# The last step of a mixture of experts: the accumulated rows read from POOL's queue, and the tokens finished in two halves

## Chip, cores, metric

The kernel runs on one core of a Trainium2 chip. The metric is the device time of one launch in microseconds (us). Three runs of the kernel before gave 2003.7, 2014.76 and 2016.17 us: a median of 2014.76 us. PE is the matmul engine, DVE the vector engine, ACT the scalar engine, POOL the GpSimd engine, and SP the queue that issues most DMAs.

## What is computed

Two blocks, one after the other, on 512 tokens of width 1024 in fp32. The first is a gated delta rule with a convolution branch and then a mixture of experts, the second a state-space mixer with a feed-forward net. The change lies where the mixture of experts ends and the second block begins:

```python
def moe_ffn(h, router_w, router_bias, w_gate, w_up, w_down, s_gate, s_up, s_down):
    ...
    out = lax.map(expert_block, (slot_tok.reshape(n_blocks, MOE_BLOCK), block_exp))
    weighted = (out.reshape(n_slots, d) * slot_w[:, None]).astype(h.dtype)
    routed = jnp.zeros((t + 1, d), h.dtype).at[slot_tok].add(weighted)[:t]
    return (routed + swiglu(hf, s_gate, s_up, s_down)).reshape(bsz, n, d)
...
        x = x + gt2 * moe_ffn(...)
    return rmsnorm(x, g_final)
...
        xn = rmsnorm_2(h, norm_mix_g[l])
```

So each token's row is the sum of its residual, its shared expert's row and the rows of six routed experts. Two norms follow at once: the first block's last, and the second block's first.

## The kernel before, in words

The 64 experts are taken in blocks of up to 128 slots (`blocks`, line 1642). For each block SP loads three tiles of 1 MB of weights per expert (`load`, line 1525), POOL gathers the tokens' rows (`gather`, line 1593), and `ffn` computes: PE turns the rows, DVE and ACT copy them out, PE multiplies gate and up (`gu`), ACT and DVE form the gated product, PE multiplies down (`py`), and DVE writes the scaled result `y` (line 1631). `scatter` (line 1639) then adds `y` to a table in DRAM: an indirect DMA that POOL issues, with addition in the DMA. There are two such tables, `yacc[0]` and `yacc[1]`, which the scatters use in turn. `yacc[0]` was filled with the residual rows at the start.

The last block has no scatter. At its place in the program the kernel does the following:

- `sums(0)` reads the table `yacc[0]` into two slots of the weights' ring (line 1686), four DMAs of 512 KB, one for each tile of 128 tokens. The remaining scatters are issued, and `sums(1)` reads `yacc[1]` in the same way.
- `ysh`, which appears in the trace as the tile `h`, holds the shared expert's rows, four tiles of 128 tokens by 1024 in SBUF. POOL adds the four tiles of the first sum to it (line 1667).
- `ffn` computes the last block, and `beyond` (line 1706) is a loop on the device for experts with more tokens than planned. Its count `nov` is read by every engine (line 1709). In this run the body is never entered, but all engines meet at its entry (line 1710), where SP first waits for the DMAs and engines whose work precedes the loop in the program.
- After the loop the second sum is added: tiles 0 and 1 by DVE, tiles 2 and 3 by POOL (line 1672). `combine` (line 1690) builds one-hot matrices `oh` from the last block's token numbers (lines 1695 and 1698), multiplies each with `y` on PE (tile `pc`, in the trace `pce`, eight of 128x512), and DVE adds each to `h` (line 1704).

Then the second block normalises `h`: ACT squares (line 2278), DVE multiplies by the norm's weight (line 2271), ACT squares that (line 2272), DVE computes the reciprocal roots, and PE turns the tiles (`ptn`) for the first product (`psi`).

A scheduler of the framework sets each engine's order within the program's dependences. Each engine runs its own list in order. A dependence is a semaphore wait in front of an instruction, so everything behind it on that engine waits as well. After the last block's weights SP has the reads of line 1686, and then the loads `wraw` and `wri` of the second block's weights (`w_in`, line 2082), which ACT and DVE split into two parts (lines 273 and 274).

## Time and profile before

| what | us |
|---|---|
| median of three runs | 2014.76 |
| the profiled execution, by its own time | 2013.86 |
| span of its trace | 2012.0 |
| from the first read of a table (1191.0) to the first `xnl` of the second block (1234.3) | 43.3 |

The profile is one execution. A timeline row gives the start in us from the span's start, the duration, the engine, the line and the operation with its tiles, output first. The chain of waits follows the work that ended last back through whatever released it. A "to landing" figure is the time from a DMA's issue to its completion.

### The profile page before, as it was taken

How to read it: one execution, taken by the hardware profiler on the slowest of the kernel's cores; microseconds unless marked ns; L12 is line 12 of the kernel's file. 1: busy time of each engine (PE TensorE's matmuls, PEld its weight loads, DVE VectorE, ACT ScalarE, POOL GpSimd, SP SyncE). 2: the span in 40 equal slices, each digit the busy share in tenths (PEclk: the TensorE clock that was granted, in tenths of full speed). 3: DMA queues.
4: the chain of work that ended last, by engine and by line, in shares of the span. 5: the costliest groups of instructions: out<-in, count | busy, mean ns of one | idle time of the engine just before them, and what ended most of it. 6: DMA issues, size and time to landing. Idle time of an engine off the chain costs nothing.

```text
span 2012.0 us, 24236 instructions
## 1 busy us (share of the span) xinstructions
PE 1832.7 (91%) x8481; PEld 1240.3 (62%) x8481; DVE 991.9 (49%) x2219; ACT 596.6 (30%) x1124; POOL 505.7 (25%) x408
## 2 busy tenths in 40 slices
PE   5897789987888999989999987999999999999998
PEld 3686557875643333333333335888888788888886
DVE  4689955667866222352222227776423453323352
ACT  5443311113423111111111114433423344323341
POOL 1314343542322222212221225342001113101300
PEclk9998889998989999999999997999999999999999
DMA  8354353226487999999999983332323423233241
GB/s 313 119 185 154 89 163 105 77 72 220 155 315 281 354 366 350 346 397 384 367 368 368 376 316 111 113 107 79 113 89 95 140 85 105 89 94 100 79 141 43
DMA packets 135555, 393.64 MB, mean 196 GB/s; under 512 B 46899, under 2 KB 59443, under 8 KB 109064
## 3 DMA queue, kind: packets, MB, share of 16 engines
q1 hardware_dynamic: 116664, 364.45, 51.2%
q0 software_dynamic: 11856, 26.83, 5.4%
q10 hardware_dynamic: 6912, 0.79, 0.3%
q8 instruction: 68, 1.11, 0.2%
q14 instruction: 55, 0.45, 0.1%
HBM read 365.19 MB, written 38.54 MB: 201 GB/s over the span
## 4 chain that ended last, share of the span: by engine, by line
PE 70%; DVE 14%; DMA 10%; ACT 3%; issue 2%; POOL 1%; SPq 0%; ACTq 0%; another core or an unknown queue 0%; DVEq 0%; POOLq 0%
PE psi L139 12%; PE gub L139 11%; PE pof L139 9%; PE psf L139 9%; PE pyb L139 7%; DMA ewrank<-ew 5%; PE psco L139 2%; DVE cfa L746 2%; PE poo L139 2%; PE pt_xb L142 1%; PE pxca L139 1%; PE psga L139 1%; PE psgb L139 1%; PE pxv L139 1%; PE psp L139 1%
## 5 line engine op out<-in xcount | busy, mean ns | idle before, releaser
L139 PE MATMUL gub<-ewrank,xTb 128*64 128x512 f32 (+5 forms) x960 | 266.3, 595 | 0.8 <-DMA ewrank<-ew 0.6
L274 DVE TENSOR_TENSOR wlo<-wraw,whi 128x1024 fp32r<-128x1024 f32 (+1 forms) x102 | 119.8, 1175 | 144.0 <-ACT whi L273 143.2
L139 PEld LDWEIGHTS gub<-ewrank,xTb 128*64 128x64 f32 (+5 forms) x960 | 88.9, 140 | 158.7 <-issue 146.1
L273 ACT CAST whi<-wraw 128x1024 fp32r<-128x1024 f32 (+1 forms) x115 | 113.9, 990 | 217.9 <-PE psi L139 50.5
L139 PE MATMUL pyb<-ewrank,hTb 128*64 128x512 f32 (+5 forms) x440 | 153.4, 612 | 2.4 <-ACT hTb L1622 0.5
L139 PE MATMUL psi<-xnh,whi 128*128 128x512 f32 (+1 forms) x368 | 141.5, 386 | 0.0
L139 PE MATMUL psi<-xnl,whi 128*128 128x512 f32 (+1 forms) x368 | 141.5, 385 | 0.0
L1617 DVE SCALAR_TENSOR_TENSOR hb<-gub,tw,sgb 128x256 f32<-128x256 f32 (+5 forms) x38 | 18.3, 482 | 229.5 <-ACT sgb L1615 229.5
L1341 ACT ACTIVATE xTb<-pt_xb,B,A 128x128 f32<-128x128 f32 (+5 forms) x168 | 74.0, 445 | 179.7 <-DVE xTb L1343 176.6
L1639 POOL DMA_INDIRECT yacc<-yb,tok x61 | 86.1, 1411 | 159.0 <-DVE yb L1631 108.3
L1593 POOL DMA_INDIRECT X<-hrow,tok x38 | 39.6, 1042 | 294.8 <-PE pt_xb L142 289.2
L139 PE MATMUL psi<-xnh,wlo 128*128 128x512 f32 (+1 forms) x296 | 113.2, 383 | 0.0
L1343 DVE TENSOR_SCALAR xTb<-pt_xb,A,B 128x128 f32<-128x128 f32 (+5 forms) x168 | 65.5, 392 | 89.2 <-PE pt_xb L142 52.0
L2433 POOL TENSOR_TENSOR fr<-fr 128x512 f32<-128x512 f32 x32 | 48.6, 1519 | 238.2 <-ACT fr L2432 238.2
L139 PE MATMUL psf<-xml,whi 128*128 128x512 f32 (+1 forms) x272 | 102.5, 377 | 0.2 <-DVE xml L274 0.2
L139 PE MATMUL psf<-xmh,whi 128*128 128x512 f32 (+1 forms) x272 | 102.5, 377 | 0.2 <-ACT xmh L273 0.2
L139 PE MATMUL psf<-xmh,wlo 128*128 128x512 f32 (+1 forms) x272 | 102.4, 377 | 0.0
L1631 DVE TENSOR_TENSOR yb<-pyb,gt 128x512 f32<-128x512 f32 (+5 forms) x84 | 57.9, 690 | 73.7 <-PE pyb L139 73.6
L139 PEld LDWEIGHTS pyb<-ewrank,hTb 128*64 128x64 f32 (+5 forms) x440 | 46.6, 143 | 74.6 <-issue 64.7
L1615 ACT ACTIVATE sgb<-gub 128x256 f32<-128x256 f32 (+5 forms) x42 | 16.0, 381 | 258.3 <-PE gub L139 258.3
L139 PEld LDWEIGHTS psi<-xnh,whi 128*128 128x128 f32 x368 | 69.6, 190 | 13.9 <-issue 0.2
L139 PEld LDWEIGHTS psi<-xnl,whi 128*128 128x128 f32 x368 | 69.7, 189 | 13.5
(755 smaller groups left out, 4041.9 us busy)
## 6 DMA issues: line engine op xcount, KB each, us to landing
ewrank<-ew SPq DMA_DIRECT2D x168, 1024.0 KB
wraw<-w_in SPq DMA_DIRECT2D x59, 512.0 KB
wraw<-ff SPq DMA_DIRECT2D x32, 512.0 KB
wf<-ff SPq DMA_DIRECT2D x64, 256.0 KB
wm<-w_mod SPq DMA_DIRECT2D x28, 512.0 KB
ewfix<-ew SPq DMA_DIRECT2D x12, 1024.0 KB
ewx<-ew SPq DMA_DIRECT2D x12, 1024.0 KB
wm<-w_mod SPq DMA_DIRECT2D x10, 1024.0 KB
```

The lines of the kernel that those rows point to most:

```text
L139: return self._done(self.eng.matmul(out, lhsT, rhs, **kw), rate, rhs)
L142: return self._done(self.eng.transpose(out, in_, ident), 0.00118, ident)
L273: nc.scalar.copy(hi, raw)
L274: (eng or nc.vector).tensor_tensor(lo, raw, hi.bitcast(F32), ALU.subtract)
L746: V.scalar_tensor_tensor(a[:, r0 * 64:r1 * 64], y[:, (r0 + o) * 64:(r1 + o) * 64], w[:, j, 15 + o:16 + o], a[:, r0 * 64:r1 * 64], ALU.mult ...
L1341: nc.scalar.activation(dst(c), pt[:, i, :], AF.Identity, scale=sa, bias=sb)
L1343: nc.vector.tensor_scalar(dst(c), pt[:, i, :], sa, sb, ALU.mult, ALU.add)
L1593: self.k.nc.gpsimd.indirect_dma_start(out=X[0:idx.shape[0]], out_offset=None, in_=self.hrow, in_offset=bass.IndirectOffsetOnAxis(ap=idx, a ...
L1617: nc.vector.scalar_tensor_tensor(h[0:n], gu[0:n, 256:512], wslot[0:n], sg[0:n], ALU.mult, ALU.mult)
L1631: nc.vector.tensor_tensor(y[0:n, cs], py[0:n], self.gt2[0:n, cs], ALU.mult)
L1639: self.k.nc.gpsimd.indirect_dma_start(out=self.yacc[1 - self.nsc % 2], out_offset=bass.IndirectOffsetOnAxis(ap=idx, axis=0), in_=y[a:a + n ...
L2433: nc.gpsimd.tensor_tensor(r, r, r, ALU.mult)
```

## The change

Both reads are issued by POOL in place of SP: two DMAs of 1 MB for each sum in place of four of 512 KB. POOL adds the first sum to tiles 0 and 1 alone. The one-hot matrices of the last block are built before its `ffn`, in the buffer of an earlier block's gathered rows (`Xt[1]`, in the listing `X_4568`). After the loop DVE adds the second sum to tiles 0 and 1, and `combine` finishes these two. Then DVE adds both sums to tiles 2 and 3, and `combine` finishes those. POOL has no addition after the loop.

```diff
--- before.py
+++ after.py
@@ -1663,14 +1663,20 @@
                 while pend:
                     self.scatter(*pend.pop(0))
                 s1 = self.sums(1)
-                for t in range(4):
+                for t in range(2):
                     self.k.nc.gpsimd.tensor_tensor(self.ysh[:, t, :], self.ysh[:, t, :], s0[t], ALU.add)
+                oh = self.ones_at(bp, self.tok[:, b:b + 1], rows, "e")
             y = self.ffn(bp, ps, ws, Xs[n], (self.twf if n < NFIX else self.tw)[:, b:b + 1], rows, f"b{b}")
             if n == len(BLOCKS) - 1:
                 self.beyond(bp, ps)
-                for t in range(4):
-                    (self.k.nc.gpsimd if t > 1 else self.k.nc.vector).tensor_tensor(self.ysh[:, t, :], self.ysh[:, t, :], s1[t], ALU.add)
-                self.combine(bp, ps, y, self.tok[:, b:b + 1], rows, "e")
+                add = lambda t, s: self.k.nc.vector.tensor_tensor(self.ysh[:, t, :], self.ysh[:, t, :], s[t], ALU.add)
+                for t in (0, 1):
+                    add(t, s1)
+                self.combine(ps, y, oh, rows, "e", (0, 1))
+                for s in (s0, s1):
+                    for t in (2, 3):
+                        add(t, s)
+                self.combine(ps, y, oh, rows, "e", (2, 3))
                 break
             part = self.parts(n)
             pend.append((y, part))
@@ -1682,26 +1688,30 @@
     def sums(self, i):
 
         s = [self.slot(f"sum{i}{j}").rearrange("p (t d) -> p t d", t=2) for j in range(2)]
-        for t in range(4):
-            self.k.nc.sync.dma_start(s[t // 2][:, t % 2, :], self.yacc[i][t * P:(t + 1) * P])
+        for j in range(2):
+            self.k.nc.gpsimd.dma_start(s[j], self.yacc[i][256 * j:256 * j + 256].rearrange("(t p) d -> p t d", p=P))
         return [s[t // 2][:, t % 2, :] for t in range(4)]
 
-    def combine(self, pool, ps, y, tok, n, nm):
-
-        nc = self.k.nc
-        V = nc.vector
+    def ones_at(self, pool, tok, n, nm):
+
+        V = self.k.nc.vector
         tf = pool.tile([P, 4], F32, tag="tf", name="tf" + nm, bufs=1)
         for t in range(4):
             V.tensor_scalar(tf[0:n, t:t + 1], tok[0:n], float(-P * t), None, ALU.add)
-        oh = pool.tile([P, 8, P], F32, tag="xT", name="oh" + nm)
+
+        oh = self.Xt[1][:, 0:4 * P].rearrange("p (t a) -> p t a", t=4)
         for t in range(4):
             V.tensor_scalar(oh[0:n, t, :], self.col0[0:n], tf[0:n, t:t + 1], None, ALU.is_equal)
-        for t in range(4):
-            for half in range(2):
-                cs = slice(512 * half, 512 * half + 512)
-                pc = ps.tile([P, 512], F32, tag=("py", "tp", "gu")[(2 * t + half) % 8 // 3], name=f"pc{nm}{t}{half}")
-                nc.tensor.matmul(pc, oh[0:n, t, :], y[0:n, cs], start=True, stop=True)
-                V.tensor_tensor(self.ysh[:, t, cs], self.ysh[:, t, cs], pc, ALU.add)
+        return oh
+
+    def combine(self, ps, y, oh, n, nm, tiles):
+
+        nc = self.k.nc
+        for i, (t, half) in enumerate([(t, half) for t in tiles for half in range(2)]):
+            cs = slice(512 * half, 512 * half + 512)
+            pc = ps.tile([P, 512], F32, tag=("py", "tp", "gu")[(2 * t + half) // 3], name=f"pc{nm}{t}{half}")
+            nc.tensor.matmul(pc, oh[0:n, t, :], y[0:n, cs], start=True, stop=True)
+            nc.vector.tensor_tensor(self.ysh[:, t, cs], self.ysh[:, t, cs], pc, ALU.add)
 
     def beyond(self, bp, ps):
         k, nc, tc = self.k, self.k.nc, self.k.tc
@@ -1721,7 +1731,7 @@
                 ws.append(t)
             X = self.gather(sl)
             y = self.ffn(bp, ps, [ws], X, sw, P, "o")
-            self.combine(bp, ps, y, sl, P, "o")
+            self.combine(ps, y, self.ones_at(bp, sl, P, "o"), P, "o", range(4))
```

The first place is POOL, from the scatter of the last block but two to the loop's entry. `yacc_67` and `yacc_68` are the two tables, `yb_8737` is the result of the last block but one, `sum_8781` and `sum_8782` hold the first sum, and `sum_8788` and `sum_8789` the second. Before:

```order
L1639 DMA yacc_67<-yb_8666,tok 512x1024
L1639 DMA yacc_68<-yb_8737,tok 512x1024
L1667 TENSOR_TENSOR h_3610<-h_3610,sum_8781 128x1024 x2
L1667 TENSOR_TENSOR h_3610<-h_3610,sum_8782 128x1024 x2
L1709 TENSOR_LOAD nov
```

Now:

```order
L1639 DMA yacc_67<-yb_8666,tok 512x1024
L1692 DMA sum_8781<-yacc_67 128x2x1024
L1692 DMA sum_8782<-yacc_67 128x2x1024
L1667 TENSOR_TENSOR h_3610<-h_3610,sum_8781 128x1024 x2
L1639 DMA yacc_68<-yb_8737,tok 512x1024
L1692 DMA sum_8788<-yacc_68 128x2x1024
L1692 DMA sum_8789<-yacc_68 128x2x1024
L1719 TENSOR_LOAD nov
```

The four reads are new here. The scatter of `yb_8737` now stands behind the first two reads and behind two additions, and the second sum's reads stand behind the scatter, ahead of the loop.

The second place is DVE, from the first addition of the second sum (`sum_8790`) behind the loop to the last addition of a `pce`. Before (four `tfe` and three `ohe` stand just ahead of the piece):

```order
L1672 TENSOR_TENSOR h_3610<-h_3610,sum_8790 128x1024
L1698 TENSOR_SCALAR ohe<-col_3645,tfe 128x128
L1672 TENSOR_TENSOR h_3610<-h_3610,sum_8790 128x1024
L1704 TENSOR_TENSOR h_3610<-h_3610,pce_9000 128x512
L1704 TENSOR_TENSOR h_3610<-h_3610,pce_9003 128x512
L1704 TENSOR_TENSOR h_3610<-h_3610,pce_9006 128x512
L1704 TENSOR_TENSOR h_3610<-h_3610,pce_9009 128x512
L1704 TENSOR_TENSOR h_3610<-h_3610,pce_9012 128x512
L274 TENSOR_TENSOR wlo<-wraw,whi 128x1024
L1704 TENSOR_TENSOR h_3610<-h_3610,pce_9015 128x512
L1704 TENSOR_TENSOR h_3610<-h_3610,pce_9018 128x512
L1704 TENSOR_TENSOR h_3610<-h_3610,pce_9021 128x512
```

Now (`sum_8782` is the first sum's part for tiles 2 and 3, `sum_8788` the second's for tiles 0 and 1):

```order
L1672 TENSOR_TENSOR h_3610<-h_3610,sum_8788 128x1024 x2
L1714 TENSOR_TENSOR h_3610<-h_3610,pce_8990 128x512
L1714 TENSOR_TENSOR h_3610<-h_3610,pce_8993 128x512
L1714 TENSOR_TENSOR h_3610<-h_3610,pce_8996 128x512
L1714 TENSOR_TENSOR h_3610<-h_3610,pce_8999 128x512
L1672 TENSOR_TENSOR h_3610<-h_3610,sum_8782 128x1024 x2
L1672 TENSOR_TENSOR h_3610<-h_3610,sum_8789 128x1024 x2
L1714 TENSOR_TENSOR h_3610<-h_3610,pce_9006 128x512
L1714 TENSOR_TENSOR h_3610<-h_3610,pce_9009 128x512
L1714 TENSOR_TENSOR h_3610<-h_3610,pce_9012 128x512
L1714 TENSOR_TENSOR h_3610<-h_3610,pce_9015 128x512
```

The four `tfe` and the four `ohe` are gone from here, as is one `wlo` (it now stands ahead of the loop). Four additions of 128x1024 that POOL did before stand in the middle.

The third place is SP, behind the last block's last weights (`ewrank_2_8779`). Before:

```order
L1525 DMA ewrank_2_8779<-ew 128x2048
L1686 DMA sum_8781<-yacc_67 128x1024 x2
L1686 DMA sum_8782<-yacc_67 128x1024 x2
L1686 DMA sum_8790<-yacc_68 128x1024 x2
L1710 COMPARE_AND_BRANCH
```

Now:

```order
L1525 DMA ewrank_2_8779<-ew 128x2048
L2092 DMA wraw<-w_in 128x1024 x2
L1720 COMPARE_AND_BRANCH
```

Six reads of the tables have gone from ahead of the loop, and two loads of the second block's weights have come up to it from behind it.

## Rows read from the trace of the kernel before

**Rows 1.** The page: busy time of PE over the span; last chain by engine.
```profile
PE 1832.7 (91%) x8481; PEld 1240.3 (62%) x8481; DVE 991.9 (49%) x2219; ACT 596.6 (30%) x1124; POOL 505.7 (25%) x408
...
PE 70%; DVE 14%; DMA 10%; ACT 3%; issue 2%; POOL 1%; SPq 0%; ACTq 0%; another core or an unknown queue 0%; DVEq 0%; POOLq 0%
```

**Rows 2.** Chain of waits, 1180 to 1235 us (start us, us, what).
```profile
1182.69 8.25 DMA yacc<-yb,tok
...
1191.00 10.46 DMA sum<-yacc
...
1207.04 2.42 another core or an unknown queue
...
1209.50 1.38 POOL h L1667
...
1211.78 10.15 PE pce L139 x16
...
1223.14 2.36 DVE h L2271 x2
```

**Rows 3.** Timeline of POOL (start us, us, engine, line, op).
```profile
1195.21 1.42 POOL L1639 DMA_INDIRECT yacc<-yb,tok  x1 [11.10 <-DVE yb L1631]
1201.60 9.26 POOL L1667 TENSOR_TENSOR h<-h,sum 128x1024 f32<-128x1024 f32 x4 [4.98 <-DMA sum<-yacc]
1214.90 4.68 POOL L1672 TENSOR_TENSOR h<-h,sum 128x1024 f32<-128x1024 f32 x2 [4.03 <-DMA sum<-yacc]
```

**Rows 4.** SP's queue: waits of line 1686, and its timeline from 1211 us.
```profile
L1686 SPq EVENT_SEMAPHORE  x3: 17/10283/10507, 1180.5 to 1192.8; - x3
...
1211.12 0.80 SPq L1686 DMA_DIRECT2D sum<-yacc  x2
```

**Rows 5.** DMAs issued by POOL: landing of line 1639's; 512 KB direct ones.
```profile
DMA to landing us min/median/max: 4.3/8.0/12.6
...
inv<-o POOLq DMA_DIRECT2D x2, 512.0 KB, 3.9
```

**Rows 6.** DMA rate, 1185 to 1225 us, 40 slices of 1 us.
```profile
GB/s 283 274 188 176 180 188 188 295 393 381 385 406 361 164 188 94 86 98 66 233 205 401 279 25 8 8 0 197 311 426 414 414 328 8 0 0 0 90 365 434
```

**Rows 7.** Timeline of DVE, 1206 to 1224 us.
```profile
1207.45 0.69 DVE L1631 TENSOR_TENSOR yb<-pyb,gt 128x512 f32<-128x512 f32 x1 [0.21 <-PE pyb L139]
1211.20 0.34 DVE L1695 TENSOR_SCALAR tfe<-tok 128x1 f32<-128x1 int32 x4 [3.06 <-POOL h L1667]
1211.45 0.67 DVE L1698 TENSOR_SCALAR ohe<-col,tfe 128x128 f32<-128x128 f32 x3
1212.03 1.22 DVE L1672 TENSOR_TENSOR h<-h,sum 128x1024 f32<-128x1024 f32 x1
...
1217.31 0.69 DVE L1704 TENSOR_TENSOR h<-h,pce 128x512 f32<-128x512 f32 x1 [1.02 <-PE pce L139]
...
1221.19 1.87 DVE L1704 TENSOR_TENSOR h<-h,pce 128x512 f32<-128x512 f32 x3
```

**Rows 8.** Timeline of PE's weight loads, 1211 to 1224 us.
```profile
1216.21 0.34 PEld L139 LDWEIGHTS pce<-yb,ohe 128*128 128x128 f32 x1 [0.52 <-issue]
1217.07 0.34 PEld L139 LDWEIGHTS pce<-yb,ohe 128*128 128x128 f32 x1 [0.52 <-issue]
```

**Rows 9.** Busy time by stretch; the eighth figure is the granted clock.
```profile
1211.00:1223.00 12.00, 10.13 (x16) 4.04 (x16) 9.59 (x19) 3.14 (x4) 4.75 (x4) 0.72 0.52 182
```

**Rows 10.** Timeline of DVE, 1223 to 1235 us.
```profile
1225.48 1.22 DVE L274 TENSOR_TENSOR wlo<-wraw,whi 128x1024 fp32r<-128x1024 f32 x1
...
1233.13 1.21 DVE L274 TENSOR_TENSOR wli<-wri,whi 128x1024 fp32r<-128x1024 f32 x1
1234.27 0.47 DVE L2299 SCALAR_TENSOR_TENSOR xnl<-ptn,vec,xnh 128x256 fp32r<-128x256 f32 x1
```

**Rows 11.** Timeline of DVE, 1176 to 1183 us.
```profile
1178.82 0.36 DVE L1343 TENSOR_SCALAR xTb<-pt_xb,A,B 128x80 f32<-128x80 f32 x1 [0.55 <-ACT xTb L1341]
1180.01 0.69 DVE L1631 TENSOR_TENSOR yb<-pyb,gt 80x512 f32<-80x512 f32 x1 [0.84 <-PE pyb L139]
```

## The prediction

> **What bounds the kernel now.** I read the page first: PE is busy for 91% of the span and has 70% of the chain that ended last [rows 1]. The change doesn't touch that work. It touches one seam, where the experts end and the second block begins, so what it can do is bounded by that seam: 43 us from the first read of a table at 1191.0 us to the first `xnl` at 1234.27 [rows 2, 10]. A difference under 1% (20 us) is about what a measurement of this kernel can't tell from no change, so even a change that halved the seam would just show.
>
> Second, the chain of waits inside the seam [rows 2]. The scatter of the last block but two is issued at 1182.69 and lands 8.25 us later. Only then can SP read table 0, and 10.46 us pass before POOL's first addition is released. POOL's four additions, 9.26 us, run from 1201.60 to 1210.86 [rows 3], and the chain goes through them to the loop's entry, where all engines meet. DVE starts again at 1211.20 [rows 7]. I call that moment M. Then come eight `pce` products, 10.15 us, whose additions on DVE end at 1221.19 + 1.87 = 1223.06 [rows 7]. I call that E. At 1223.14 the norm's multiplications begin [rows 2]. So M is set by POOL, and E - M = 11.9 us by PE and DVE.
>
> Third, what ran beside this and was hidden. The last scatter went out at 1195.21, when POOL had nothing to do [rows 3]. SP began to wait for it at 1192.8 and waited 10.3 to 10.5 us, so it landed near 1203.2, about 8.0 us after its issue [rows 4]. The first half of the second sum was read behind that. Its second half was issued only after the loop, at 1211.12 [rows 4], and POOL had it at 1214.90 [rows 3]. The rate of the DMAs in the slices from 1204 to 1207 shows the first half passing [rows 6]. All of that ended before POOL's additions did. In the changed kernel it doesn't.
>
> **The change part by part.** *The new chain on POOL.* POOL's list now has: read table 0, two additions, last scatter, read table 1, loop. Each of these waits for the one ahead, for its data or simply for its place.
>
> - Start: the first read still waits for the scatter of 1182.69, so it is issued near 1191.0.
> - Landing of the first 1 MB. Below, 3.9 us, the 512 KB that POOL wrote from a queue of its own [rows 5]; above, the 10.46 us of SP's read, which stood behind the tail of the last weights and beside the last scatter. I take 8.0, nearer the upper row, since the weights' tail and now two `wraw` loads are still under way, while the last scatter is not.
> - Two additions in place of four: 2 x 9.26 / 4 = 4.6 us. POOL is at 1203.6.
> - The last scatter, ready at 1195, goes out there, 8.4 us later than before. From issue to landing 61 scatters took 4.3 to 12.6 us, with a median of 8.0 [rows 5], the same as this one took before. I take 8.0: 1211.6.
> - The 2 MB of table 1: 3.9 us for the first 512 KB, then 1.57 MB at the 0.41 MB/us that the better slices show [rows 6], 3.8 us: 7.7 us, to 1219.3. Below, 3.9; above, 10.5 as for SP's read. All of it now stands ahead of the loop, so the loop's entry waits for it; before, half of it came after.
> - From the last thing that the entry waits for to DVE's start 0.3 us (1210.86 to 1211.20): M = 1219.6, against 1211.2, +8.4 us. Below, M can't come before about 1210: the last `yb` ends at 1208.1 [rows 7], and a `wlo` of 1.2 us [rows 10] has moved behind it, ahead of the loop. That is -1.2. Above, 1191.0 + 10.5 + 4.6 + 12.6 + 10.5 + 0.3 = 1229.5, +18.3.
>
> The Trainium skill (DMA: Bandwidth & Descriptors, "Issuing engine by pattern" and the table of specifications) sends plain loads to SP's queue and gives a first byte after about 1 us from POOL's against 0.6 us from SP's. Two of the reads stand on the chain, so by that page, as an estimate, 0.8 us would be added. No row here shows one transfer from both queues. The same page ("Queues, rings and completion order") lets each DMA engine go round its queues packet by packet. By that the first 1 MB would share the engines with SP's loads instead of queueing behind them, and would land sooner than my 8.0, which the 10.46 us of a read in SP's own queue neither shows nor excludes.
>
> *From M to E.* DVE before: eight small operations, two additions, eight `pce` additions and one `wlo`. PE paced it: one `pce` is two passes, 0.86 us apart [rows 8], 1.7 us in all, at a mean granted clock of 0.72 after its idle time [rows 9], between the levels of 1.2 and 2.4 GHz. Now `oh` is ready, so PE starts at M. DVE needs 2 x 1.2 = 2.4 us for the second sum of tiles 0 and 1 and then follows PE: the third `pce` was added 5.5 us after PE's start (1211.78 to 1217.31 [rows 2, 7]), the fourth comes within 1.2 to 1.7 more, and its addition ends at about M + 7.6. Then come four additions of 128x1024, at the 2.36 / 2 of the norm's multiplications, which are the same shape [rows 2]: 4.7 us, M + 12.3. PE has meanwhile finished, so the last four additions follow each other at 1.87 / 3 = 0.62 [rows 7]: 2.5 us. E = M + 14.8, that is +2.9 us. Two of these additions were POOL's before the loop, and two were POOL's beside PE after it; both kinds were covered, and now DVE pays. Below, were PE at its full clock from the start: 2.4 + 2.5 + 4.7 + 2.5 = 12.1, +0.2. Above, one more us where DVE and PE fall out of step: +3.9.
>
> *Building `oh` early.* Four operations of 0.67 / 3 = 0.22 us [rows 7] go into DVE's gaps of 0.55 and 0.84 us about 1180 [rows 11]: nothing. With that cover gone it is 0.9 us.
>
> *Finishing two tiles first.* ACT's plain squares of tiles 0 and 1 can start some 7 us before E. But the multiplication by the norm's weight stands behind the last `pce` on DVE in the new order, and the roots need squares of its result. So I count nothing. Two of the `wlo` and `wli` splittings of 1.2 us [rows 10] change places around the roots: one that delayed the first `xnl` now delays the roots. Nothing, with 1 us either way.
>
> *SP freed.* The `wraw` loads come some 35 us earlier. PE doesn't wait for these weights in the seam, so nothing.
>
> **The sum.** +8.4 + 2.9 = +11.3 us against the profiled execution's own 2013.86 (span 2012.0 and 1.9 around it): 2025.2 us. The median of the runs shown is 0.9 above that execution, and one run is 11 below. The ends of the terms give -1.2 + 0.2 - 1.0 = -2.0 and 18.3 + 3.9 + 1.0 + 0.9 = +24.1.
>
> **The rivals.**
>
> *Everything lands late (slower by over 1%).* The scatter and both reads of tables now run one after the other on one queue while SP's second-block loads use the same DMA engines. If all three take the upper rows, M = 1229.5 and with +2.9 the time is 2013.86 + 21.2 = 2035.1. For it: the scatters' spread up to 12.6. Against it: at the late scatter and the last reads little else is in flight.
>
> *A quiet queue (not slower).* POOL's reads don't stand behind SP's weights, and the late scatter finds the engines empty and lands like the fastest of the 61. Then M is at its floor of 1210, -1.2, and with PE warm E - M is 12.1: -1.0 us in all, 2012.9. It decides once the three waits sum to no more than 1211.0 - 0.3 - 4.6 - 1191.0 = 15.1 us, where I take 23.7. For it: POOL wrote 512 KB in 3.9 us. Against it: a scatter of this size took 8 us at the median, and PE idles longer than before, not shorter.
>
> *The halves do overlap (the reverse of what I read).* If the norm's first two multiplications, 2.36 us, fell into DVE's waits for PE, the time would be 2022.8. The order speaks against it: they stand behind all `pce` additions.
>
> **How the numbers follow.** Forecast (between 2016 and 2033) 0.65, late landing 0.15, quiet queue 0.13, overlap 0.03, anything outside the seam 0.04. The range from 2010 to 2036 takes in most of the terms' ends and leaves out about 2 in 10 with the spread of the runs. Faster by over 1% is below 1994.6, which none of the cases reaches: 0.03. Slower by over 1% is above 2034.9, a part of the late landing: 0.09. The rest, 0.88, is within 1%.
>
> **What would show it.** POOL's last scatter near 1203.6 in place of 1195.2; the reads of table 1 issued near 1211.6; the loop left near 1219.6; four additions of 128x1024 on DVE between the fourth and the fifth `pce`; E about 14.8 us behind M; the first `xnl` some 11 us later. It is wrong if the scatter still goes out ahead of POOL's additions, if the three waits sum to 15 us or less, or if a difference of more than 5 us arises outside 1177 to 1250 us.

## The result, and the profile after

The changed kernel takes 2031.55 us, the median of six runs (2023.24 to 2033.81), against 2013.4 us for six runs of the kernel before: the medians lie 18 us apart. The ratio on record, which is not the plain quotient of the medians, is 1.0081, with a 95% interval of 1.0065 to 1.0096: slower by 0.8%, some 16 us. The forecast was 2025.2 us, slower by 11.3 us. The profiled execution of the changed kernel has a span of 2029.3 us, 17.3 more than before.

The page first, its busy time and its last chain by engine:

```profile
PE 1837.0 (91%) x8481; PEld 1242.0 (61%) x8481; DVE 994.1 (49%) x2223; ACT 596.4 (29%) x1124; POOL 500.5 (25%) x408
...
PE 70%; DVE 16%; DMA 9%; ACT 3%; issue 2%; POOL 1%; SPq 0%; DVEq 0%; ACTq 0%; POOLq 0%
```

No engine's busy time moved by more than some 5 us against [rows 1]. What the kernel lost, it lost waiting. The timeline of POOL shows where, from the scatter of the last block but two on:

```profile
1184.83 1.42 POOL L1639 DMA_INDIRECT yacc<-yb,tok  x1 [9.32 <-DVE xTb L1343]
1193.73 1.59 POOL L1692 DMA_DIRECT2D sum<-yacc  x2 [7.47 <-DMA ewrank<-ew]
1204.66 4.67 POOL L1667 TENSOR_TENSOR h<-h,sum 128x1024 f32<-128x1024 f32 x2 [9.35 <-DMA sum<-yacc]
1209.50 1.54 POOL L1639 DMA_INDIRECT yacc<-yb,tok  x1 [0.17 <-DVE yb L1631]
1216.30 1.50 POOL L1692 DMA_DIRECT2D sum<-yacc  x2 [5.26 <-issue]
```

Read the starts downwards: each is one link of POOL's new list. The last scatter leaves at 1209.50, 24.7 us behind the first row; before it left 12.5 us behind it (1195.21 [rows 3] against 1182.69 [rows 2]). The chain of waits then follows this list into the loop's entry (start us, us, what):

```profile
1209.50 1.54 POOL yacc L1639
...
1217.05 7.50 DMA sum<-yacc
...
1224.62 0.04 POOLq L1720
...
1225.61 0.10 POOL cv L2342
...
1225.84 6.79 PE pce L139 x8
...
1233.33 3.46 DVE h L1672 x4
...
1240.26 2.27 DVE h L2281 x2
```

In [rows 2] the DMA in this place was that of table 0; now it is table 1's, 26 us later. DVE's timeline from the loop on:

```profile
1225.71 2.36 DVE L1672 TENSOR_TENSOR h<-h,sum 128x1024 f32<-128x1024 f32 x2 [14.29 <-POOL cv L2342]
1227.98 0.68 DVE L1714 TENSOR_TENSOR h<-h,pce 128x512 f32<-128x512 f32 x1
...
1232.65 0.69 DVE L1714 TENSOR_TENSOR h<-h,pce 128x512 f32<-128x512 f32 x1 [0.60 <-PE pce L139]
1233.25 4.62 DVE L1672 TENSOR_TENSOR h<-h,sum 128x1024 f32<-128x1024 f32 x4
1237.79 2.47 DVE L1714 TENSOR_TENSOR h<-h,pce 128x512 f32<-128x512 f32 x4
...
1250.17 0.48 DVE L2309 SCALAR_TENSOR_TENSOR xnl<-ptn,vec,xnh 128x256 fp32r<-128x256 f32 x1
...
1260.62 3.22 DVE L2309 SCALAR_TENSOR_TENSOR xnl<-ptn,vec,xnh 128x256 fp32r<-128x256 f32 x8 [1.44 <-ACT xnh L2308]
```

DVE sits idle for 14.29 us; in [rows 7] it waited 3.06. Then the four additions of 128x1024 (4.62 us) stand between the fourth and the fifth `pce`, on the path. The kernel before had the last row's counterpart, `xnl` of the second half of the tokens, here:

```profile
1243.47 3.22 DVE L2299 SCALAR_TENSOR_TENSOR xnl<-ptn,vec,xnh 128x256 fp32r<-128x256 f32 x8 [2.62 <-ACT xnh L2298]
```

That instruction is a good ruler. From it to the end of the span all thirteen profiled executions of this study (before, after and the eleven below) take between 768.4 and 769.3 us. So I measure everything from S, the issue of the scatter of the last block but two, to this `xnl`, which I call X. X - S was 60.78 us and is 75.79: the seam lost 15.0. S itself is 2.1 us later in the profile after, though nothing on PE's path ahead of it changed, and S lies between 1180.9 and 1187.7 in those thirteen executions. I take that for variation from one execution to the next, which is why a single span is a poor ruler for a change of this size. The ruler has a limit too: it is read from one execution of each kernel. In ten of the eleven kernels with a ratio, the ratio puts the difference to before 0.3 to 3.4 us higher than X - S does. No run shows whether that arises ahead of S or is chance in the one trace of the kernel before.

### The profile page after: what moved, and what is told of

Read it like the earlier page. It is cut to its first block, busy times and chain, and to the rows that moved or that the text cites. A ratio compares the mean times of both kernels' runs of the same rounds, so it can differ in the third digit from the quotient of the medians.

```text
span 2029.3 us, 24238 instructions
## 1 busy us (share of the span) xinstructions
PE 1837.0 (91%) x8481; PEld 1242.0 (61%) x8481; DVE 994.1 (49%) x2223; ACT 596.4 (29%) x1124; POOL 500.5 (25%) x408
## 4 chain that ended last, share of the span: by engine, by line
PE 70%; DVE 16%; DMA 9%; ACT 3%; issue 2%; POOL 1%; SPq 0%; DVEq 0%; ACTq 0%; POOLq 0%
PE psi L139 12%; PE gub L139 11%; PE pof L139 9%; PE psf L139 9%; PE pyb L139 6%; DMA ewrank<-ew 6%; PE psco L139 2%; DVE cfa L746 2%; PE poo L139 2%; DVE gt L569 1%; PE psga L139 1%; PE psgb L139 1%; PE pxca L139 1%; PE pt_xb L142 1%; PE sg L139 1%
```

## The experiments

M is again DVE's first operation behind the loop, E the end of the last `pce` addition. All variants compute everything. Ratios are to the kernel before, with 95% intervals; M - S and X - S are of one profiled execution each. `pin` in an edit keeps an operation at its place in the program's order.

| kernel | ratio | M - S | X - S |
|---|---|---|---|
| before | - | 28.5 | 60.8 |
| after | 1.0081 [1.0065, 1.0096] | 40.9 | 75.8 |
| ones early alone | 1.0004 [0.9992, 1.0016] | 28.1 | 59.1 |
| after, reads on SP | 1.0013 [1.0002, 1.0024] | 27.3 | 62.3 |
| after, scatter first | 1.0062 [1.0040, 1.0083] | 36.9 | 71.8 |
| after, four additions: two ahead of the loop | 1.0068 [1.0050, 1.0087] | 40.8 | 72.3 |
| after, second block's weights late | 1.0073 [1.0052, 1.0094] | 41.5 | 78.8 |
| before, reads on POOL alone | 1.0128 [1.0108, 1.0148] | 43.8 | 83.2 |
| before, products ahead of the loop | 1.0015 [1.0004, 1.0027] | 34.3 | 62.6 |
| the same, DVE adds the whole second sum | 0.9998 [0.9983, 1.0012] | 34.3 | 60.1 |
| the same, second sum ahead of the loop | 1.0020 [1.0008, 1.0033] | - | 62.3 |
| the same, its tiles exchanged | 1.0009 [0.9998, 1.0020] | - | 59.5 |

(In the last two nothing of the sums is left behind the loop, so M has no meaning.) The intervals of the changed kernel and of the three versions with the scatter first, with two additions ahead of the loop, and with the late weights overlap. What differs among these four is read from the traces alone.

**Is it POOL's list? The changed kernel with its reads back on SP.**

```diff
-        for j in range(2):
-            self.k.nc.gpsimd.dma_start(s[j], self.yacc[i][256 * j:256 * j + 256].rearrange("(t p) d -> p t d", p=P))
+        for t in range(4):
+            self.k.nc.sync.dma_start(s[t // 2][:, t % 2, :], self.yacc[i][t * P:(t + 1) * P])
```

> The changed kernel with both tables read by SP again, in four DMAs of 512 KB each; the halves, the early oh and POOL's two additions stay. Theory (the loss sits in POOL's list, which runs read, additions, scatter and read one behind the other): the last scatter goes out at S + 12.5 again, M - S falls from 40.9 to about 27, E - M stays near 14.5 since the second table is now read behind the loop; the time is within 3 us of before, ratio 0.999 to 1.0015. Rival (the loss comes from finishing the tokens in two halves on DVE): the time stays 10 us or more above before, ratio over 1.005.

The timeline of POOL:

```profile
1184.72 1.42 POOL L1639 DMA_INDIRECT yacc<-yb,tok  x1 [9.31 <-DVE xTb L1343]
1197.24 1.42 POOL L1639 DMA_INDIRECT yacc<-yb,tok  x1 [11.10 <-DVE yb L1631]
1203.61 4.65 POOL L1667 TENSOR_TENSOR h<-h,sum 128x1024 f32<-128x1024 f32 x2 [4.95 <-DMA sum<-yacc]
```

The scatter leaves 12.5 us behind the first row again, DVE starts at S + 27.3, and the ratio falls to 1.0013. About 14 of the 16 us are the queue. The edit also goes back to four DMAs for each table, so by itself it doesn't separate the queue from the size of the DMAs; what moved in the trace is POOL's order. The first 512 KB of the first sum still take 10.6 us from the issue to POOL's addition, about as long as the first 1 MB from POOL's queue (10.9), so the long first read doesn't come from POOL's queue.

**The reverse: only the reads moved, in the kernel before.**

```diff
-        for t in range(4):
-            self.k.nc.sync.dma_start(s[t // 2][:, t % 2, :], self.yacc[i][t * P:(t + 1) * P])
+        for j in range(2):
+            self.k.nc.gpsimd.dma_start(s[j], self.yacc[i][256 * j:256 * j + 256].rearrange("(t p) d -> p t d", p=P))
```

> The kernel before with only the reads moved to POOL's queue, two of 1 MB for each table; POOL adds all four tiles of the first sum, oh is built behind the loop, no halves. POOL's list now has three additions ahead of the last scatter and one behind it. Theory (POOL's list is the loss): scatter at S + 27, M - S = 43, E - M about 12.5; ratio to before 1.007 to 1.009, as the whole change. Rival (the halves and DVE's additions are most of the loss): ratio under 1.004.

Alone it costs 1.28%, some 26 us (2039.3 against 2013.76 us), where 0.7 to 0.9% were forecast. The scatter (S + 26.8) and M came as expected, but E - M was 17.0 us in place of 12.5. So the rest of the change, taken together, gives about 10 us back by the ratio (7.4 by X - S): POOL's two additions fewer, no addition on POOL behind the loop, and `oh` ready. The timeline behind the loop shows where the forecast of E failed:

```profile
1224.70 5.62 POOL L1672 TENSOR_TENSOR h<-h,sum 128x1024 f32<-128x1024 f32 x2 [7.76 <-issue]
...
1224.77 6.62 DVE L1672 TENSOR_TENSOR h<-h,sum 128x1024 f32<-128x1024 f32 x2 [16.09 <-issue]
```

DVE's two additions of 128x1024 take 6.62 us here, beside two on POOL. In the changed kernel two take 2.36. More on this below.

**Only the ones early, in the kernel before.** `combine` is split as in the change, the rest stays.

> The kernel before, with only the one-hot matrices built early, in the buffer of gathered rows. Times are counted from S, the issue of the scatter of the last block but two; M is DVE's first operation behind the loop, E the end of the last pce addition. Before: M - S 28.5 us, E - M 11.9. Theory (early oh is free and worth little): M - S stays 28.5, E - M falls to about 11, since PE starts 0.6 us sooner; the time falls by 1 us, ratio 0.9995. Rival (the four early operations delay the last but one block on DVE and PE): the scatter after S goes out 1 us later and the time rises by 1 us.

No measurable difference (1.0004): as the prediction said, it is hidden. E - M fell to 10.7 us, but 1 us is too little for the ratio to show. The trace has the first read of a table, issued by SP at 1193.96, landing 10 us later, again. It also shows that this is the landing of 512 KB, one tile, since POOL had to wait for the second tile as well:

```profile
1203.91 2.34 POOL L1667 TENSOR_TENSOR h<-h,sum 128x1024 f32<-128x1024 f32 x1 [4.30 <-DMA sum<-yacc]
1206.44 6.96 POOL L1667 TENSOR_TENSOR h<-h,sum 128x1024 f32<-128x1024 f32 x3 [0.18 <-DMA sum<-yacc]
```

The first 1 MB was there at 1206.44, 12.5 us after the issue. From POOL's queue the first 1 MB took 10.9 us in the changed kernel.

**The scatter ahead of POOL's additions, in the changed kernel.**

```diff
+                for t in range(2):
+                    pin(self.k, self.k.nc.gpsimd.tensor_tensor(self.ysh[:, t, :], self.ysh[:, t, :], s0[t], ALU.add))
                 s1 = self.sums(1)
-                for t in range(2):
-                    self.k.nc.gpsimd.tensor_tensor(self.ysh[:, t, :], self.ysh[:, t, :], s0[t], ALU.add)
```

> The changed kernel with POOL's order mended: the last scatter stands ahead of the two additions, the second table's reads behind them. Theory (order on POOL): scatter at S + 12.5, first table landed at S + 20, additions to S + 24.5, second table read from there in 8.3 us, M - S = 34 in place of 40.9; E - M unchanged at 14.5; the time falls by 7 us against the changed kernel, ratio to before 1.0045. Rival (reads from POOL's queue are slow in themselves, and more so beside the scatter): the first table lands 3 us later still, M - S 37 or more, ratio 1.006 or more.

```profile
1187.65 1.42 POOL L1639 DMA_INDIRECT yacc<-yb,tok  x1 [9.32 <-DVE xTb L1343]
1196.33 1.60 POOL L1692 DMA_DIRECT2D sum<-yacc  x2 [7.26 <-DMA yacc<-yb,tok]
1200.18 1.54 POOL L1639 DMA_INDIRECT yacc<-yb,tok  x1 [2.25 <-DVE yb L1631]
1207.41 4.67 POOL L1666 TENSOR_TENSOR h<-h,sum 128x1024 f32<-128x1024 f32 x2 [5.69 <-DMA sum<-yacc]
1215.02 1.47 POOL L1692 DMA_DIRECT2D sum<-yacc  x2 [2.94 <-issue]
```

It came out between the two forecasts: M is 4 us earlier, not 7, and the ratio, 1.0062, is the rival's. The scatter went out at S + 12.5, as wanted, but table 1 could be read only at 1215.02, 14.8 us after it (1200.18); in the changed kernel these are 6.8 us. By the trace's landing figures the scatter landed 13.0 us after its issue here, and 1.8 us more passed before POOL issued the read. With the reads on SP the scatter at S + 12.5 landed in 7.7 us, and in the kernel before with the reads on POOL alone, where it goes out when both reads have landed, in 5.8. Here it stood behind 2 MB of reads in the same queue, with the `wraw` loads in flight as well. That the place behind the reads held it back fits these figures, but no run changed that place alone. So the queue had two prices: what POOL may issue next, and when what it issued gets through.

**Two of the four additions ahead of the loop, in the changed kernel.**

```diff
+                for t in (2, 3):
+                    pin(self.k, self.k.nc.vector.tensor_tensor(self.ysh[:, t, :], self.ysh[:, t, :], s0[t], ALU.add))
                 self.beyond(bp, ps)
...
-                for s in (s0, s1):
-                    for t in (2, 3):
-                        add(t, s)
+                for t in (2, 3):
+                    add(t, s1)
```

> The changed kernel with the first sum of tiles 2 and 3 added by DVE ahead of the loop, where DVE waits for M, in place of between the fourth and the fifth pce. Theory (each addition of 128x1024 behind the loop is paid in full on DVE): M - S stays 40.9, E - M falls by 2.3 to 12.2; ratio to before 1.007. Rival (DVE follows PE there, and additions are hidden): E - M falls by less than 1 us.

```profile
1209.65 2.35 DVE L1672 TENSOR_TENSOR h<-h,sum 128x1024 f32<-128x1024 f32 x2
...
1225.10 2.36 DVE L1674 TENSOR_TENSOR h<-h,sum 128x1024 f32<-128x1024 f32 x2 [11.96 <-issue]
...
1231.42 2.35 DVE L1674 TENSOR_TENSOR h<-h,sum 128x1024 f32<-128x1024 f32 x2
```

The first row lies in DVE's idle time, M stays, and E - M falls from 14.6 to 11.1 us: 2.3 for the two additions, and 1.2 since PE's third and fourth product came 0.86 us apart in this execution. The four additions cost what the prediction put on them.

**Why does the first read take 11 us? The second block's weights held back, in the changed kernel.** A read of 128x4 of table 1 by SP, behind the last scatter, is put ahead of the `wraw` loads.

```diff
                 s1 = self.sums(1)
+                self.k.hold = self.k.nc.sync.dma_start(bp.tile([P, 4], F32, name="hold", bufs=1), self.yacc[1][0:P, 0:4])
...
-    k.nc.sync.dma_start(raw, src)
+    q = k.nc.sync.dma_start(raw, src)
+    if nm in ("i0", "i1"):
+        k.tc.add_manual_dep(q.ins, k.hold.ins.name, mybir.DependencyInfo(mybir.DependencyClass.NoSync, mybir.DependencyReason.DATA), reason="behind the last scatter")
```

> The changed kernel with SP's first two loads of the second block's weights held back behind a small read (128x4) of the second table, so behind the last scatter. Theory (the first read of 10.9 us is slow because these 1 MB and the weights' tail share the DMA engines with it): it lands in about 8 us, M - S falls by 3 to 38. Rival (it is slow by the lagging engines that the scatters and the experts' weights leave behind, or by POOL's queue itself): it still takes 10 us or more, and M - S stays at 40 to 41.

The first read landed 10.3 us after its issue instead of 10.9. The theory that the `wraw` loads make it long fell: they are worth 0.6 us at most. Held back, they then ran beside the read of table 1, and M - S was 41.5 against 40.9. X - S grew by 3.0 us, 2.6 of them behind E, where DVE now has a `wlo` that stands ahead of the loop in the changed kernel. The ratio doesn't show these 3 us.

**The same question, answered: the reads in quiet.** All four reads wait until POOL has copied 128x4 of the last block's result; the last scatter goes first.

```diff
-                s0 = self.sums(0)
                 while pend:
                     self.scatter(*pend.pop(0))
...
+                self.gate = self.k.nc.gpsimd.tensor_copy(bp.tile([P, 4], F32, name="gate", bufs=1)[0:rows], y[0:rows, 0:4])
+                s0 = self.sums(0)
                 s1 = self.sums(1)
...
+            self.k.tc.add_manual_dep(q.ins, self.gate.ins.name, mybir.DependencyInfo(mybir.DependencyClass.NoSync, mybir.DependencyReason.DATA), reason="behind the gate")
```

> The changed kernel with the last scatter first and all four reads of the tables on POOL's queue held back until POOL has copied 128x4 of the last block's result: they are issued near 25 us after the scatter of the last block but two, when the last block's weights and both scatters have long landed. All of it is still computed; it isn't meant to be fast. Measured: the time from the issue of the first read to POOL's first addition, 10.9 us in the changed kernel and 10 to 11 in each version so far, from either queue, with or without the second block's weights, with or without the last scatter beside it. Theory: what makes it long is the tail of the last block's weights, which some of the DMA engines still have before them when the read is issued (the rate falls to a third for the read's last 5 us). Then the first 1 MB lands 5 to 6.5 us after its issue here, and the rate stays near 0.4 MB/us to the end. Rival: it is long by itself (the first read of a table, or of rows just scattered). Then 10 to 11 us here as well. The norm's multiplication starts near 55 us by the theory, near 60 by the rival.

```profile
1211.92 1.60 POOL L1693 DMA_DIRECT2D sum<-yacc  x2 [0.62 <-PEq L1722]
1214.51 1.42 POOL L1693 DMA_DIRECT2D sum<-yacc  x2 [0.98 <-issue]
1217.85 4.63 POOL L1671 TENSOR_TENSOR h<-h,sum 128x1024 f32<-128x1024 f32 x2 [1.92 <-DMA sum<-yacc]
```

The first addition starts 5.93 us after the read's issue, in place of 10.93. The busy share of the DMA engines (in tenths) and their rate show why, first in the changed kernel from 1190 us (40 slices of 1 us), then in this one from 1200 us (40 of 0.75):

```profile
DMA  6655498999953322100007460003799996002798
GB/s 188 188 209 242 184 258 311 393 406 430 410 201 123 127 115 98 49 29 8 0 16 49 66 119 0 0 0 33 152 414 422 410 426 250 0 0 49 254 406 348
```

```profile
DMA  3776321000000000056999999999999999980000
GB/s 126 170 180 180 87 60 38 22 22 0 0 0 0 0 0 0 0 55 76 366 415 421 415 393 431 432 421 393 415 426 404 404 410 410 393 317 27 0 11 0
```

In the changed kernel the DMAs run at 400 GB/s for four slices (1197 to 1200) and then at 100 to 200 for five, with a busy share that falls from 9 tenths to between 5 and 2: the rest seems to hang on a few engines. Ahead of the read the engines were only half busy (the 6, 5 and 4 from 1190 on) at about 200 GB/s, which suggests that the weights' tail lay on some engines and not on others; what the read had on the former would come last. In quiet the 4 MB, and 1 MB of `wraw` beside them, pass at about 400 GB/s to the end. So what was in flight at S + 9 costs the first read some 5 us, and SP's queue doesn't spare it. The `wraw` loads and the last scatter are excluded by the other versions. That the table's rows had just been written is excluded by table 1, which POOL read right behind its scatter in the changed kernel, 2 MB in 8.25 us. The weights' tail is what is left. The busy shares fit that, though no run took the tail alone away. The kernel as a whole was no faster for it (2032.35 us in one run, before 2015.07), since the reads began 16 us later.

**A better order? The products ahead of the loop, in the kernel before with the ones early.**

```diff
-                self.beyond(bp, ps)
+                self.combine(ps, y, oh, "e")
+                self.beyond(bp, ps)
                 for t in range(4):
                     (self.k.nc.gpsimd if t > 1 else self.k.nc.vector).tensor_tensor(self.ysh[:, t, :], self.ysh[:, t, :], s1[t], ALU.add)
-                self.combine(ps, y, oh, "e")
```

> The kernel before (SP reads, four additions of the first sum on POOL) with oh built early and all eight pce and their additions ahead of the loop, beside the last scatter and the second table's reads. Theory (the pce stand on the chain only because they come behind the loop, and PE is still at its full clock there): PE runs them from S + 25.6 in 7 us, DVE has added the last by S + 33.5, M - S is about 34 in place of 28.5, and the norm's first operation starts at S + 36.5 in place of 40.4: 4 us less than before, ratio 0.998. Rival (the loop's entry now waits longer and the second table's second half, read ahead of it, sets M): the norm starts at S + 40 or later, ratio 1.000 or more.

```profile
1216.28 5.63 POOL L1674 TENSOR_TENSOR h<-h,sum 128x1024 f32<-128x1024 f32 x2 [4.89 <-DVEq L1716]
1217.50 5.49 DVE L1674 TENSOR_TENSOR h<-h,sum 128x1024 f32<-128x1024 f32 x2 [1.82 <-issue]
```

The eight products were hidden as planned and M came as the theory said (S + 34.3), but the gain didn't come: DVE's two additions took 5.49 us beside POOL's, which took 5.63. DVE's two alone take 2.36, POOL's two 4.67. The norm's multiplication began at S + 39.7, where 36.5 was expected and 40.5 was before, and X - S is longer than before, 62.6. The ratio, 1.0015, is what the rival had, for another reason than the rival's.

**Do the engines slow each other? DVE adds all four tiles.**

```diff
-                    (self.k.nc.gpsimd if t > 1 else self.k.nc.vector).tensor_tensor(self.ysh[:, t, :], self.ysh[:, t, :], s1[t], ALU.add)
+                    self.k.nc.vector.tensor_tensor(self.ysh[:, t, :], self.ysh[:, t, :], s1[t], ALU.add)
```

> The version that finished the last block's eight products ahead of the loop, with one edit: DVE adds the second sum to all four tiles behind the loop, and POOL adds nothing there. In that version DVE's two additions took 5.49 us (2.36 where nothing ran beside them) and POOL's two took 5.63 (4.67 alone). Theory: two additions with both inputs in SBUF, one on DVE and one on POOL at the same time, slow each other. Then DVE's four additions take 4.7 us, and the norm's first multiplication starts 39.0 us after the issue of the scatter of the last block but two (39.74 in that version, though DVE does twice the work); ratio to before 0.999 to 1.002. Rival: DVE's additions were slow for another reason of the place (data still landing, the memory where the sum lies). Then four take 9 to 11 us, and the multiplication starts at 43 to 45; ratio 1.003 to 1.005.

```profile
1218.23 4.63 DVE L1674 TENSOR_TENSOR h<-h,sum 128x1024 f32<-128x1024 f32 x4 [1.82 <-issue]
```

Yes: DVE makes all four additions in 4.63 us, less than its two took beside POOL's. The multiplication starts at S + 38.9 (39.0 expected).

**Everything ahead of the loop, and then the tiles exchanged.** In the first version POOL adds the second sum to tiles 2 and 3 and DVE to 0 and 1, in the second it is the other way round. The edit shown is the second's, against the version with the products ahead of the loop; the first has the tiles in the order 2, 3, 0, 1 and the two engines exchanged:

```diff
-                self.beyond(bp, ps)
                 for t in range(4):
-                    (self.k.nc.gpsimd if t > 1 else self.k.nc.vector).tensor_tensor(self.ysh[:, t, :], self.ysh[:, t, :], s1[t], ALU.add)
+                    pin(self.k, (self.k.nc.vector if t > 1 else self.k.nc.gpsimd).tensor_tensor(self.ysh[:, t, :], self.ysh[:, t, :], s1[t], ALU.add))
+                self.beyond(bp, ps)
```

> The same version, but all of the second sum's additions stand ahead of the loop, POOL's (tiles 2 and 3) behind its four of the first sum, DVE's (tiles 0 and 1) behind the eight additions of the products; the reads stay on SP. Theory: with POOL's list free of reads nothing of this chain waits for a late transfer. POOL is through near 33 us after the issue of the scatter of the last block but two, DVE near 35, the additions don't meet one of the other engine with both inputs in SBUF, the loop is left near 36, and the norm's first multiplication starts there (before 40.45): ratio 0.997 to 0.999. Rival: the second half of the second sum's read, which SP issues only near 22 us, lands after 33 us; then POOL and DVE wait for it ahead of the loop, the additions run side by side and slow each other, and the multiplication starts at 40 or later: ratio 1.000 to 1.002.

> The version with all additions ahead of the loop, with the second sum's tiles exchanged: POOL adds tiles 0 and 1, whose products DVE has added first, and DVE adds tiles 2 and 3 behind its last product. Theory: then POOL works from 28.0 to 32.7 us after the issue of the scatter of the last block but two, beside DVE's additions of products (one input of which lies in PSUM, 0.69 us each whether POOL adds or not), and DVE's two additions run from 32.4 to 34.8, when POOL is through. No two additions with both inputs in SBUF meet, so POOL's two take 4.7 us in all (5.63 when they met), DVE's two 2.4 (5.21), and the norm's first multiplication starts near 36.6 us (39.35 in that version, 40.45 before). Ratio to before 0.997 to 1.000. Rival: an addition on POOL is slowed by DVE's additions of products too, or the second sum's second half lands late; then POOL's end after 34 us, the additions meet again, and the multiplication starts at 39 or later: ratio 1.000 to 1.003.

The timelines, of the first:

```profile
1216.92 5.63 POOL L1673 TENSOR_TENSOR h<-h,sum 128x1024 f32<-128x1024 f32 x2 [3.43 <-DVE h L1710]
...
1218.42 5.21 DVE L1673 TENSOR_TENSOR h<-h,sum 128x1024 f32<-128x1024 f32 x2
```

and of the second:

```profile
1213.79 4.67 POOL L1673 TENSOR_TENSOR h<-h,sum 128x1024 f32<-128x1024 f32 x2
1213.81 1.48 DVE L1710 TENSOR_TENSOR h<-h,pce 128x512 f32<-128x512 f32 x2 [0.24 <-PE pce L139]
...
1218.64 2.35 DVE L1673 TENSOR_TENSOR h<-h,sum 128x1024 f32<-128x1024 f32 x2
```

In the first, POOL had to wait for DVE's products of tiles 2 and 3 (3.43 us), so the additions met after all; I had overlooked that dependence. The multiplication started at S + 39.35, where 36 was forecast, and the ratio, 1.0020, is the rival's. In the second they are apart, and both take their short time. The multiplication starts at S + 36.5 (36.6 expected), 4 us earlier than before. Even so the ratio is 1.0009, just past the 1.000 at which the forecast ended, with an interval that holds 1.000. Of the 4 us 1.6 are left at the first `xnl` and 1.3 at X. Behind the second half's multiplication DVE had one splitting of 1.21 us before; now it has a `wlo` that takes 2.06 us beside POOL, and more of the second half's small operations ahead of the first `xnl`. What was won at the norm's start was mostly given back a few rows later. No version here beats the kernel before by a measurable amount.

## Why the prediction was right, and where it was short

**The direction and the cause.** It named POOL's list as the new chain and the loop's entry as the place where it bites. Reads back on SP removed 14 of 16 us; reads on POOL alone cost 26. This is shown by both directions of the same edit. How much was lost came out less well: the seam lost 15.0 us where 11.3 were forecast. The prediction also took 1% for about what a measurement here can't tell from no change; the interval of the ratio is 0.15% to either side.

**The terms of M.** The sum was made of six links. Their measures, from POOL's timeline and the chain above:

| link | forecast us | measured us | from |
|---|---|---|---|
| S to the first read's issue | 8.3 | 8.9 | 1184.83 to 1193.73 |
| landing of the first 1 MB | 8.0 | 10.9 | to 1204.66 |
| two additions | 4.6 | 4.8 | to 1209.50 |
| scatter, to the next read's issue | 8.0 | 6.8 | to 1216.30 |
| 2 MB of table 1 | 7.7 | 8.25 | to 1217.05 + 7.50 |
| loop's entry | 0.3 | 1.2 | to 1225.71 |
| M - S | 36.9 | 40.9 | |

Before, M - S was 28.5, so M lost 12.4 where 8.4 was forecast. The mis-sized step is "Landing of the first 1 MB ... I take 8.0". It said itself that the weights' tail was still under way, and then chose a value below the one row, 10.46 us, that had that tail in it, because the last scatter would be gone. That row is moreover the landing of one tile, 512 KB; the first 1 MB took SP 12.5 us in the version with the ones early alone. In the changed kernel the scatter was gone and the read still took 10.9 us, so the scatter is not what made that row long. In quiet it took 5.9, so what was left of the loads did. The prediction's thought that sharing the engines with SP's loads would land the 1 MB sooner than 8.0 us did not come out. The second mis-sized step is the entry: "0.3 us" was read from a case where POOL came in with an addition. In the chain above POOL steps through a row of waits of L1720 between the landing (1217.05 + 7.50 = 1224.55) and its way out, and DVE starts 1.2 us after the landing. In two of the versions with the products ahead of the loop DVE needed 1.8 us from its last work ahead of the loop to its first behind it. One row is too few for such a price. The scatter's term came out 1.2 us short, and that is luck in part: where the landing can be read (the version with the scatter first, and the kernel before with the reads on POOL alone), some 1.8 us pass between it and the issue of table 1's read, a wait that the sum didn't have. The landing itself was then nearer 5 us than 8.0 (an estimate, 6.8 less 1.8).

**From M to E.** 14.55 us (1225.71 to 1240.26), forecast 14.8. DVE's four additions in the middle took 4.62, forecast 4.7. Two of them moved ahead of the loop gave 2.3 us back.

**Building `oh` early, and SP freed.** Costed at nothing, and the ratios of the ones alone and of the held-back weights show no difference. By the X ruler the early weights are worth up to 3 us against the version that holds them back, though against the kernel before X - E didn't move.

**Two tiles first.** Counted at nothing, and X - E is 20.4 us before and after. ACT's timeline shows the early squares of tiles 0 and 1, and what then has to wait:

```profile
1230.38 1.06 ACT L2288 ACTIVATE nj<-h 128x1024 f32<-128x1024 f32 x1 [3.86 <-DVE h L1714]
...
1241.43 1.06 ACT L2282 ACTIVATE nk<-h 128x1024 f32<-128x1024 f32 x1 [5.98 <-DVE h L2281]
```

The plain square (`nj`) is 10 us ahead of E. The square of the multiplied tile (`nk`) waits for the multiplication behind all `pce`, just as the order said. The first `xnl` came 13.8 us later behind S than before, where some 11 were forecast.

**The rivals.** "Everything lands late" overstated two links of three: the first read did land late, beyond the 10.46 us of its upper row, while the scatter and table 1 met nearly empty engines, as the argument against it held. "A quiet queue" wanted the three waits in 15.1 us; they took 26.0 (10.9 + 6.8 + 8.25). The seam's loss is 12.4 + 2.7 = 15.1, and the X ruler gives 15.0.

## What to carry to other kernels

Moving a DMA to another queue moves everything behind it on that queue: write that queue's new list down, link by link, and ask which link another engine must now wait for. A transfer's time belongs to its moment as much as to its size: take the duration from a row of the same size with the same neighbours in flight. And before giving half of an addition to a second engine, look whether both halves are ever seen side by side in a trace at their single durations.

## What the hardware showed that I had not expected

In these traces DVE and POOL didn't add two SBUF operands at once but took turns. Side by side DVE's two additions took 5.49, 6.62 and 5.21 us in three kernels (2.36 alone) and POOL's two 5.63, 5.62 and 5.63 (4.67 alone). From the first start to the last end that is 6.7 us each time (1216.28 to 1217.50 + 5.49 = 1222.99 in the first), close to the 4.67 + 2.36 = 7.0 of doing one after the other. One by one, in the version with the products ahead of the loop, POOL's first ends at 1218.62, DVE's first, begun at 1217.50, at 1219.70, POOL's second, begun at 1218.58, at 1221.91, and DVE's second at 1222.99. So each ends about its own single time (1.2 us on DVE, 2.3 on POOL) after the other engine's last. The Trainium skill (SBUF — State Buffer, "SBUF: two separate sides") says that a GpSimd operation that reads SBUF and a DVE operation with two SBUF inputs take turns at a shared pair of ports, each holding it for a whole instruction; the trace agrees with taking turns by whole additions (1.1 and 2.2 us after the other's end). Additions of a `pce`, one of whose inputs lies in PSUM, keep their pace (1.48 us for two) beside POOL, and POOL its 4.67. In the kernel before this stayed hidden because POOL's data came late (4.03 us idle at 1214.90 [rows 3]), after DVE was done with its two.

POOL's queue seems to have kept a scatter back as well: behind 2 MB of reads it landed in 13.0 us, and in 5.8 where both reads had landed. In both versions table 1's read left POOL some 1.8 us after that landing; by the trace of the kernel before, SP issued its read of table 1 within 0.1 us of it.
